# Two edits in the S5 stage of a diffusion block on one core: the state-space mixer's local table stays on the chip, and the modulation weights of the MLP scale are summed by TensorE ahead of the gated unit

## The chip, the cores and the metric

The kernel runs on one core of one Trainium2 chip. A core has five engines with instruction queues of their own: TensorE (PE in the rows; its weight loads are listed apart as PEld), VectorE (DVE), ScalarE (ACT), GpSimd (POOL) and SyncE (SP), which here only issues DMAs. Each queue is worked off in order. The metric is the device time in microseconds (us), median of several runs.

## What is computed

One block for a latent stream x of 256 tokens x 2048 channels, with a context of 256 tokens. Everything is float32, and the matrix weights are read once. Cut to what is run here:

```
sh1, sc1, gt1, sh2, sc2, gt2 = split(silu(c) @ w_mod + b_mod, 6)     # w_mod: 2048 x 12288; c_ctx the same
h = modulate(rmsnorm(x), sh1, sc1);   h_ctx likewise
# S5 mixer: 128 groups of 16 channels, 64 complex states per group, two directions
bu = einsum(u, b_bar);  states = scan(lam_bar, bu)                    # context first, then latent
y  = u * d + sum over directions of einsum(states, c_mat).real
a, g = split(gelu(y) @ w_glu);   m = a * sigmoid(g)                   # w_glu: 2048 x 4096
x = x + gt1 * rmsnorm(m)
h = modulate(rmsnorm(x), sh2, sc2)
x = x + gt2 * rmsnorm(relu(h @ w1)^2 @ w2)                            # 2048 x 8192, 8192 x 2048
```

The sixth of w_mod that gives sc2, the scale of the MLP's modulation, is one of the six 2048 x 2048 parts, 16 MB. The kernel calls it kind 4. Kinds 0 and 1 (the mixer's shift and scale, for c and c_ctx) are its "a" items, kind 2 is the mixer's gate, kind 3 the MLP's shift, kind 5 the MLP's gate.

## The kernel before

**Stages.** First the S5 stage, then the gated unit, then the MLP. The S5 stage works on 16 blocks `b` of 8 groups each, in three units of 4, 6 and 6 blocks (`UNITS`); a unit's recurrence runs as one scan. Weights come as items of 1 MB through one ring of tiles `raw` with three buffers (`RAWBUFS`), in one fixed order: 32 "a" items, then 32 "k" items of the kinds 3 and 2 between which the first ten items of the gated unit ("g", `GLU_EARLY`) are mixed (`MIX[n]` says how many k items stand before g item n), then 22 more g items, then the MLP. The ten early g items are multiplied in float32 straight from `raw`. The other 22 are split into a high and a low part by ScalarE and VectorE (`hi`, `lo`) and multiplied as three faster products; this is called the split stage below.

**One block of the S5 stage.** Its input tile `xv` (tiles xz0 to xz3, 4 blocks each) is multiplied with the row scale `rs` (`xn_blk`, L565) and then modulated with `vec` (`u_blk`, L569, two operations), once the "a" items of its chunk have been summed by TensorE (`a_mm`) and brought into columns (`vec_ev`, `vec_tr`, `vec_mask`, `vec_sel`, `vec_fin`). Chunks are 8, 8, 16, 32, 32 and 32 groups wide, so the last chunk feeds the last four blocks. From the discretised weights `bcb` come sums `s1e`, `s2e` (`e_sums`), and from these five operations of 512 elements per half block (`e_op`: k, e, e, and two sums), TensorE's transposes `tr`, ScalarE's copy `et`, and the matmul `v` (`v_mm`) that gives the scan its input. The scan is the chain `t`, `lat`, `lat` on VectorE (L727, L732, L734). After it ScalarE copies states (`sp_copy`), GpSimd adds two of them (`sp_sum`), VectorE makes three tables per half block (`d_op`, tiles dx), and TensorE makes the output `y` (`out_mm`) from the states and from the block's local response. `gelu` and the transpose `z_tr` follow.

**The local response.** It is a Toeplitz table: 15 diagonals of 16x16 per group. TensorE makes a strip from `e` and the block-diagonal output weights `cbd` (`strip`, L631), ScalarE copies it to `sk`, TensorE transposes it (`w_tr`), ScalarE and VectorE place it in `W` (`w_ev`, `w_diag`), SyncE writes `W` to DRAM (`w_out`) and reads it back eight times with a shift (`load_it`, 8 DMAs of 128 KB for each pair of blocks), and `out_mm` multiplies the tile `it` with `xv`.

**Engines.** Helper lines hide the work: every two-input operation made by `tt` stands at L122, every ScalarE copy at L125. In the S5 stage GpSimd does the row scale, the modulation of blocks 2 to 15, both kinds of sums and the last powers of the transition (`cmul(GP, ...)`).

**Kind 4.** Its 16 MB are loaded in the split stage into the two tiles xz0 and xz1 (`k4_load`), summed by VectorE with 16 operations of 2048 elements (`acc_op`, `acc_add`), and reduced over the partitions after the last split product by TensorE (`sc2_mm`, L1140), ScalarE (`row_ev`), TensorE (`col_mm`) and VectorE (`sc2_fin`).

**Order.** The order on each engine is fixed when the program is built: `Plan` takes all tasks with a cost, a priority, dependences and rings (counts of free buffers), simulates the engines, and emits each task when it is started in that simulation. A cost or ring that changes moves other tasks too.

Of the kernel before, what the change touches and what calls it, by code (L numbers as in the profile page):

```python
# [27 lines left out]
RAWBUFS = 3  # L28
# [9 lines left out]
MIX = (24, 26, 27, 29, 30, 32, 32, 32, 32, 32)  # L38
K4POS = ()
UNITS = (4, 6, 6)  # L40
PI = math.pi
# [75 lines left out]
def _body(ctx, tc, nc, I, O):  # L117
# [22 lines left out]
    shc = const.tile([128, 4, 4], F32, name="shc")  # L140

# [11 lines left out]

    k4v = KT - len(K4POS)
    kq = [kitem(kind, kt) for kind in (3, 2) for kt in range(KT)]
    nk = 0
    for n in range(len(GLU_ORDER)):
        m = MIX[n] if n < GLU_EARLY else nk + 2
        items += kq[nk:m]
        nk = max(m, nk)  # L160
        items.append(gitem(n))
        for j, at in enumerate(K4POS):
            if at == n:
                items.append(kitem(4, k4v + j))
# [64 lines left out]
    with psx:  # L229
# [15 lines left out]
        m16 = sb.tile([64, H], F32, name="m16")  # L245
        dcol = sb.tile([64, 32], F32, name="dcol")
# [34 lines left out]
        for dst, src in ((m16, "m16"), (dcol, "dcol"), (bcol, "bcol"), (sel4, "sel4")):  # L281
            S.dma_start(dst, I[src])
        V.memset(cst, 0.0)
        V.memset(epst, EPS)
        sk = ew.tile([128, L, 4, H], F32, name="sk")
        cbd = [ew.tile([128, 8, 2, 32], F32, name=f"cbd{n}") for n in range(2)]
        for t in cbd:
            GP.memset(t, 0.0)
# [42 lines left out]
        cm = {V: tmp("c0", [128, NB, 4, 8]), GP: tmp("c1", [128, NB, 4, 8])}  # L331
# [31 lines left out]
        cmul(GP, at(p_, 2), at(p_, 0), at(p_, 1))  # L363
        cmul(GP, span(p_, 4, 8), span(p_, 0, 4), rept(p_, 3, 4))
# [76 lines left out]
        def close_pre():  # L441
            nonlocal lp_, wk, drp
# [19 lines left out]
        for n in range(RB, min(nq + RB, len(items))):  # L462
            rawt[n] = add("SP", 2.91, lambda n=n: load_to(n + 1), prio=2, take=("raw",), lag=1.3)
# [1017 lines left out]
```

## Time and profile before

| | us |
|---|---|
| median of 3 runs (1309.31 to 1315.62) | 1313.72 |
| profiled execution | 1313.43 |
| its span, first to last instruction | 1311.7 |
| S5 stage with the early gated-unit items | 0 to 436 |
| of it up to the last step of the last scan | 0 to 386.9 |
| split stage of the gated unit | 436 to 559.3 |
| between gated unit and MLP | 559.3 to 586 |
| first MLP product | 586 to 943 |
| second MLP product and end | 943 to 1311.7 |

The boundaries are read from the timelines: where TensorE's first split product, the first product of the MLP and the first of its second half start. A row of a timeline gives start, duration, engine, line and tiles; a row of stretches gives the busy time of each engine between two times. Operations of one engine can overlap by a little in the rows, so the distance from start to start is what one costs (its pitch below), and the printed duration is longer.

### The profile page before, as it was taken

What the parts mean: (1) busy time and instruction counts of PE and PEld (TensorE: products, weight loads), DVE (VectorE), ACT (ScalarE), POOL (GpSimd) and SP (SyncE); (2) the same over time, 40 slices, a digit from 0 to 9 for tenths busy, and PEclk for the clock granted to TensorE, in tenths of its full rate; (3) what the DMA queues carried; (4) which work ended last, traced back from release to release, by engine and by line L of the source; (5) the groups of instructions that cost most, each with busy time, mean ns of one, the idle gap of its engine ahead of it and who ended that gap; (6) DMA issues with size and microseconds to landing.
All of it is one profiled execution on the core that took longest, in us unless ns stands there. A gap on an engine that the chain in (4) does not pass through costs nothing.

```text
span 1311.7 us, 22524 instructions
## 1 busy us (share of the span) xinstructions
PE 1178.7 (90%) x9457; PEld 957.2 (73%) x9457; DVE 897.1 (68%) x1200; ACT 539.4 (41%) x731; POOL 192.5 (15%) x200
## 2 busy tenths in 40 slices
PE   4576884696898999989999999999999999999997
PEld 1454553452434688989999999999978888888885
DVE  8999999878878677765555565555655555655555
ACT  5442544242115534574333334333434444444443
POOL 4766344611322000030000000000000000000000
PEclk8588997798899999999999999999999999999998
DMA  7488868989986888816656666566656555555552
GB/s 269 148 213 295 316 245 195 307 307 196 260 227 168 319 346 324 317 66 224 234 219 245 217 220 250 209 242 223 230 189 224 192 193 184 182 185 188 192 192 97
DMA packets 74093, 296.68 MB, mean 226 GB/s; under 512 B 7164, under 2 KB 30588, under 8 KB 48520
## 3 DMA queue, kind: packets, MB, share of 16 engines
q1 hardware_dynamic: 73992, 295.25, 66.3%
q8 instruction: 74, 1.21, 0.4%
q14 instruction: 27, 0.22, 0.1%
HBM read 291.15 MB, written 4.07 MB: 225 GB/s over the span
## 4 chain that ended last, share of the span: by engine, by line
PE 74%; DMA 9%; DVE 5%; SPq 1%; ACT 1%; issue 1%; POOL 0%; DVEq 0%; POOLq 0%; ACTq 0%
PE m L1325 27%; PE o L1358 27%; PE gb L998 9%; DMA raw<-wk 4%; PE gb L991 3%; DMA it<-wd 2%; DMA raw<-wa 2%; DVE e L122 2%; SPq L689 1%; PE ada L484 1%; PE y L800 1%; PE v L706 1%; DMA bcc<-bc 1%; PE m L1247 1%; PE ada L476 1%
## 5 line engine op out<-in xcount | busy, mean ns | idle before, releaser
L122 DVE TENSOR_TENSOR wlo<-raw,whi 128x2048 fp32r<-128x2048 f32 x126 | 288.7, 2291 | 134.7 <-ACT whi L125 134.7
L1325 PE MATMUL m<-h,whi 128*128 128x256 f32 x1984 | 248.2, 283 | 0.0
L125 ACT ACTIVATE whi<-raw 128x2048 fp32r<-128x2048 f32 (+1 forms) x130 | 243.8, 1876 | 1.5 <-PE m L1247 1.5
L1325 PEld LDWEIGHTS m<-h,whi 128*128 128x128 f32 x1984 | 242.5, 192 | 0.0
L1358 PE MATMUL o<-wlo,hh 128*128 128x512 f32 x512 | 160.5, 395 | 0.2 <-DVE wlo L122 0.2
L1358 PE MATMUL o<-whi,hh 128*128 128x512 f32 x512 | 160.6, 395 | 0.0
L1358 PE MATMUL o<-whi,hl 128*128 128x512 f32 x512 | 160.5, 395 | 0.0
L1325 PE MATMUL m<-h,wlo 128*128 128x256 f32 x992 | 129.1, 283 | 0.0
L1325 PEld LDWEIGHTS m<-h,wlo 128*128 128x128 f32 x992 | 123.5, 192 | 0.0
L125 ACT ACTIVATE hh<-hid 128x512 fp32r<-128x512 f32 x64 | 40.5, 633 | 194.5 <-PE o L1358 194.5
L125 ACT ACTIVATE r<-m 128x256 f32<-128x256 f32 x64 | 24.6, 384 | 222.9 <-PE m L1325 221.1
L1358 PEld LDWEIGHTS o<-wlo,hh 128*128 128x128 f32 x512 | 95.9, 187 | 24.1 <-DVE wlo L122 0.6
L1358 PEld LDWEIGHTS o<-whi,hh 128*128 128x128 f32 x512 | 95.8, 187 | 24.2 <-ACT hh L125 0.8
L1358 PEld LDWEIGHTS o<-whi,hl 128*128 128x128 f32 x512 | 96.0, 187 | 23.5
L1297 DVE TENSOR_TENSOR hl<-hid,hh 128x512 fp32r<-128x512 f32 x64 | 44.3, 693 | 88.8 <-ACT hh L125 88.7
L1269 DVE TENSOR_TENSOR hid<-r,m 128x256 f32<-128x256 f32 x64 | 26.9, 421 | 91.9 <-ACT r L125 91.9
L991 PE MATMUL gb<-raw,xz 128*128 128x512 f32 x160 | 76.0, 623 | 2.4 <-DMA raw<-wg 2.3
L623 PE MATMUL tr<-ident,e 128*128 128x128 f32 x256 | 44.7, 315 | 30.9 <-DVE e L122 24.6
L998 PE MATMUL gb<-hi,zs 128*128 128x512 f32 (+1 forms) x288 | 70.1, 357 | 0.0
L484 PE MATMUL ada<-raw,cst 128*32 128x512 f32 x256 | 36.9, 654 | 35.4 <-DMA raw<-wk 35.4
L623 PEld LDWEIGHTS tr<-ident,e 128*128 128x128 f32 x256 | 32.5, 160 | 45.8 <-DVE e L122 21.4
L991 PEld LDWEIGHTS gb<-raw,xz 128*128 128x128 f32 x160 | 30.2, 197 | 46.5 <-issue 40.2
(202 smaller groups left out, 1613.2 us busy)
## 6 DMA issues: line engine op xcount, KB each, us to landing
raw<-w SPq DMA_DIRECT2D x128, 1024.0 KB, 4.8
raw<-wk SPq DMA_DIRECT2D x48, 1024.0 KB, 8.4
raw<-wa SPq DMA_DIRECT2D x32, 1024.0 KB, 7.4
raw<-wg SPq DMA_DIRECT2D x32, 1024.0 KB, 5.2
k<-wk SPq DMA_DIRECT2D x16, 1024.0 KB, 7.3
it<-wd SPq DMA_DIRECT2D x64, 128.0 KB, 6.9
xz<-xs SPq DMA_DIRECT2D x4, 1024.0 KB, 9.1
bcb<-bc SPq DMA_DIRECT2D x16, 128.0 KB, 8.9
```

The lines of the kernel that those rows point to most:

```text
L122: eng.tensor_tensor(out=out, in0=a, in1=b, op=op)
L125: A.activation(out=out, in_=in_, func=f, **kw)
L476: PE.matmul(adab["a"][32 * j:32 * j + 32, :n], cst[:, 2 * kt:2 * kt + 32], w[:, e, j], start=(kt == 0), stop=(kt == KT - 1))
L484: PE.matmul(adab["k"][32 * j:32 * j + 32, :], cst[:, 2 * kt:2 * kt + 32], w[:, j * 512:(j + 1) * 512], start=(kt == k0), stop=(kt == KT - ...
L623: PE.transpose(est["ps"][:, gi * 128:(gi + 1) * 128], e[:, r, gi].rearrange("p s h -> p (s h)"), ident)
L689: S.dma_start(it[16 * s:16 * s + 16], wdt[b2][:, :, (7 - s) * H:(7 - s) * H + 128])
L991: PE.matmul(banks[p][nk * t + k], xz[kt // BQ][:, GQ * C + (kt % BQ) * T + t * 128:][:, :128], wt[:, (nk * e + k) * 512:(nk * e + k + 1) * ...
L998: PE.matmul(banks[p][nk * t + k][:, :wd], a, w[:, (nk * e + k) * wd:(nk * e + k + 1) * wd], start=ff, stop=ll)
L1269: V.tensor_tensor(out=hid[:, nt], in0=r, in1=ps, op=ALU.mult)
L1297: V.tensor_tensor(out=hl, in0=hid[:, 2 * i:2 * i + 2], in1=hh.bitcast(F32), op=ALU.subtract)
L1325: PE.matmul(ps, w[a][:, kt], (h2h, h2l)[b][:, kt], start=a == b == kt == 0, stop=a == 1 and kt == KT - 1)
L1358: PE.matmul(banks[nh][2 * t + k], w[2 + x][:, e, zz], w[y][:, e * 1024 + k * 512:e * 1024 + k * 512 + 512], start=f and n == 0 and e == es ...
```

## The change

- **Kind 4 becomes 16 more raw items.** They stand after kinds 3 and 2 in the list of k items, so that they are all loaded and multiplied ahead of the first split item, by `k_mm` like the others, four matmuls each. Row copy, `col_mm` and `sc2_fin` follow in the S5 stage. The loads into xz0 and xz1, VectorE's 16 sums and the reduction after the split stage are gone. `MIX` spreads the early g items over 48 k items.
- **RAWBUFS is 4** instead of 3.
- **The local response stays on the chip.** `strip` multiplies with zero-padded weights `cz` (one buffer), so that both halves of a block add up in one PSUM bank with all 15 diagonals; a matmul of a diagonal `dg` with `dsel` brings the skip term d. ScalarE copies the bank (`ext_ev`), TensorE makes the eight shifted copies by transposes (`t_tr`), ScalarE brings them into `it` (`t_ev`), and `yl_mm` multiplies at once with the block's `xv`; `yl_ev` writes the result over that half of `xv`. `out_mm` later adds it with one identity matmul. The strip, the transposes and `yl` of all blocks share one PSUM bank (`st`). The DRAM write and the 64 read-back DMAs are gone, as are `sk`, `W` and their copies.
- **GpSimd's work in the S5 stage goes to VectorE**: `xn_blk`, `u_blk`, `e_sums`, `d_sums`, `sp_sum` and the last powers. Some signs are turned so that sums replace differences.
- `gelu` comes after the transpose instead of before; the dx ring has 3 buffers instead of 4, k1 2 instead of 1, hf 2 instead of 4.
- The planner's costs of many tasks are changed.

```diff
-RAWBUFS = 3
+RAWBUFS = 4
...
-MIX = (24, 26, 27, 29, 30, 32, 32, 32, 32, 32)
-K4POS = ()
+MIX = (24, 26, 28, 32, 36, 40, 44, 48, 48, 48)
...
-    k4v = KT - len(K4POS)
-    kq = [kitem(kind, kt) for kind in (3, 2) for kt in range(KT)]
+    kq = [kitem(kind, kt) for kind in (3, 2, 4) for kt in range(KT)]
...
-            t = add("Pool", 1.23, lambda b=b: xn_blk(b), prio=3 + b, ready=28.7)
-            on_v = b < 2
-            ut[b] = add("DVE" if on_v else "Pool", 1.33 if on_v else 2.05, lambda b=b, e=V if on_v else GP: u_blk(b, e), [t, vect[chunk_of[b]]],
-                        prio=0 if on_v else 2 + b)
+            t = add("DVE", 0.61, lambda b=b: xn_blk(b), prio=PR["xn"])
+            ut[b] = add("DVE", 1.33, lambda b=b: u_blk(b, V), [t, vect[chunk_of[b]]], prio=PR["u"])
...
-            s1 = ew.tile([128, L, 8], F32, tag="s1e", bufs=2, name="s1e")
-            tt(SE, s1, Qr[:, b], Qi[:, b], ALU.add)
             s2 = ew.tile([128, 2, 8, H], F32, tag="s2e", bufs=1, name="s2e")
             tt(SE, s2[:, 0], Bv[:, 0], Bv[:, 1], ALU.add)
             tt(SE, s2[:, 1], Bv[:, 0], Bv[:, 1], ALU.subtract)
+            s1 = ew.tile([128, L, 8], F32, tag="s1e", bufs=2, name="s1e")
+            V.scalar_tensor_tensor(out=s1, in0=Qr[:, b], scalar=-1.0, in1=Qi[:, b], op0=ALU.mult, op1=ALU.subtract)
...
             k1, e = est[b, hf]
-            if k < 3:
-                o, p, c = ((k1, s1, Bv[:, 0]), (e[:, 1], Qr[:, b], s2[:, 0]), (e[:, 0], Qi[:, b], s2[:, 1]))[k]
-                tt(V, o, p[:, :, hs].rearrange("p t g -> p g t").unsqueeze(3).to_broadcast(n), c[:, hs].unsqueeze(2).to_broadcast(n), ALU.mult)
-            else:
-                tt(V, e[:, k - 3], k1, e[:, k - 3], ALU.subtract)
+            if k > 2:
+                tt(V, e[:, k - 3], k1, e[:, k - 3], ALU.add)
+                return
+            o, p, c = ((k1, s1, Bv[:, 0]), (e[:, 0], Qi[:, b], s2[:, 1]), (e[:, 1], Qr[:, b], s2[:, 0]))[k]
+            tt(V, o, p[:, :, hs].rearrange("p t g -> p g t").unsqueeze(3).to_broadcast(n), c[:, hs].unsqueeze(2).to_broadcast(n), ALU.mult)
...
+        def dg_op(b):
+            est["dg"] = dg = sb.tile([128, 128], F32, tag="dg", bufs=1, name="dg")
+            act(dg, ident, scale=dcol[:, b:b + 1])
+
         def strip(b, hf):
-            e = est[b, hf][1]
-            est["st", b, hf] = st = pst("st", 1)
-            for r in range(2):
+            k1, e = est[b, hf]
+            if hf == 0:
+                est["st", b] = pst("st", 1)
+                PE.matmul(est["st", b][:, :15 * H], est["dg"], dsel.rearrange("p s h -> p (s h)"), start=True, stop=False)
+            st = est["st", b]
+            for n, (r, w) in enumerate(((0, e[:, 0]), (1, e[:, 1]), (2, k1))[:3 if (b, hf) in PE_SUMS else 2]):
+                for d in range(2):
+                    for j in range(4):
+                        PE.matmul(st[32 * j:32 * j + 32, 7 * H * d:7 * H * d + 128], cz[:, d, r, j, hf * H:hf * H + 32], w[:, j].rearrange("p s h -> p (s h)"),
+                                  start=False, stop=(hf == 1 and n == (2 if (b, hf) in PE_SUMS else 1) and d == 1))
+
+        def ext_ev(b):
+            est["x1", b] = x = ew.tile([128, 15 * H], F32, tag="x1", bufs=2, name="x1")
+            act(x, est.pop(("st", b))[:, :15 * H], scale=-1.0)
+
+        def t_tr(b, th):
+
+            est["tp", b, th] = ps = pst("st", 1, "tp")
+            for i in range(4):
+                t = 4 * th + i
+                PE.transpose(ps[:, i * 128:(i + 1) * 128], est["x1", b][:, (7 - t) * H:(7 - t) * H + 128], ident)
+
+        def t_ev(b, th):
+            if th == 0:
...
+            act(est["it", b][:, 4 * th:4 * th + 4].rearrange("p t g h -> p (t g h)"), est.pop(("tp", b, th)))
...
+        def yl_mm(b):
+
+            est["yl", b] = ps = pst("st", 1, "yl")
+            yv = ps[:, :256].rearrange("p (t e h) -> p t e h", e=2, h=H)
+            for e in range(2):
                 for j in range(4):
-                    PE.matmul(st[32 * j:32 * j + 32, :128], cbd[b % 2][:, hf * 4 + j, r], e[:, r, j].rearrange("p s h -> p (s h)"),
-                              start=(r == 0), stop=(r == 1))
-
-        def strip_ev(b, hf):
-            lp = 2 * (b % 2) + hf
-            act(sk[:, :, lp], est.pop(("st", b, hf))[:, :128].rearrange("p (s h) -> p s h", h=H))
...
-        def w_tr(b2, hs):
...
-                PE.transpose(ps[:64, si * 128:si * 128 + 128], sk[:, s].rearrange("p l h -> p (l h)"), ident)
...
-        def w_ev(b2, hs):
...
-        def dd_mul(b2):
...
-        def w_diag(b2):
...
-        def w_out(b2):
-            wdt[b2] = wd = drp.tile([H, 16, 240], F32, tag="wd", bufs=8, name="wd")
-            S.dma_start(wd.rearrange("h (l j) f -> l h (j f)", l=4), wst[b2].rearrange("p j t h -> p (j t h)"))
-
...
-        def load_it(b2):
-            r = it_ring(b2)
-            itab[b2] = it = (lp_ if r == "it" else tail["whl"]).tile([128, 16, 128], F32, tag=r, bufs=1, name="it")
-            for s in range(L):
-                S.dma_start(it[16 * s:16 * s + 16], wdt[b2][:, :, (7 - s) * H:(7 - s) * H + 128])
+                    gi = 2 * j + e
+                    PE.matmul(yv[32 * j:32 * j + 32, :, e, :], xv[b // BQ][:, 0, (b % BQ) * 8 + gi], est["it", b][:, :, 2 * (gi % 4) + gi // 4, :], start=True, stop=True)
+
+        def yl_ev(b):
+            act(xv[b // BQ][:, 0, (b % BQ) * 8:(b % BQ) * 8 + 8].rearrange("p g c -> p (g c)"), est.pop(("yl", b))[:, :256])
...
-            sp, it = spt.pop(b), itab[b2]
+            sp = spt.pop(b)
...
+            PE.matmul(yb[b2][:, 256 * w:256 * w + 256], ident, xv[b // BQ][:, 0, (b % BQ) * 8:(b % BQ) * 8 + 8].rearrange("p g c -> p (g c)"), start=True, stop=False)
```

Where the order has changed, at three places. **VectorE right after the row scale is known.** Before, in this place (k and e: first block's tables; ARS: powers of the transition):

```order
L398 RECIPROCAL rs<-rs 128x64
L122 TENSOR_TENSOR k_319<-s1e,bcb 128x512
L122 TENSOR_TENSOR e<-Qr,s2e 128x512
L122 TENSOR_TENSOR e<-Qi,s2e 128x512
L429 COPY ARS<-pr 128x128
L430 COPY ARS<-pi 128x128
L122 TENSOR_TENSOR e<-k_319,e 128x512 x2
L438 COPY ARS<-ARS 128x128
L439 TENSOR_SCALAR ARS<-ARS 128x128
L122 TENSOR_TENSOR k_403<-s1e,bcb 128x512
```

and GpSimd at the same time (xz: the input blocks; rs: row scale; vec: modulation; s1e, s2e, s1d, s2d: sums for the tables):

```order
L122 TENSOR_TENSOR xz_75<-xz_75,rs 128x2x256 x4
L122 TENSOR_TENSOR s1e<-Qr,Qi 128x64
L122 TENSOR_TENSOR s2e<-bcb 128x128 x2
L122 TENSOR_TENSOR xz_76<-xz_76,rs 128x2x256 x4
L122 TENSOR_TENSOR xz_77<-xz_77,rs 128x2x256 x4
L122 TENSOR_TENSOR xz_78<-xz_78,rs 128x2x256
L122 TENSOR_TENSOR s1e<-Qr,Qi 128x64
L122 TENSOR_TENSOR s2e<-bcb 128x128 x2
L122 TENSOR_TENSOR xz_78<-xz_78,rs 128x2x256
```

Now, VectorE (pr, pi, c: powers; r and vec: modulation columns):

```order
L399 RECIPROCAL rs<-rs 128x64
L123 TENSOR_TENSOR xz_76<-xz_76,rs 128x2x256 x4
L123 TENSOR_TENSOR xz_77<-xz_77,rs 128x2x256 x4
L123 TENSOR_TENSOR xz_78<-xz_78,rs 128x2x256 x2
L510 TENSOR_TENSOR r_397<-vp,m_65 64x8 x4
L123 TENSOR_TENSOR xz_78<-xz_78,rs 128x2x256 x2
L522 TENSOR_TENSOR vec<-vp,rb 128x16 x2
L523 SCALAR_TENSOR_TENSOR vec<-vec,rb 128x16
L123 TENSOR_TENSOR xz_79<-xz_79,rs 128x2x256
L123 TENSOR_TENSOR xz_76<-xz_76,vec 128x2x256 x2
L123 TENSOR_TENSOR xz_79<-xz_79,rs 128x2x256 x3
L123 TENSOR_TENSOR s2e<-bcb 128x128 x2
```

The row scale of all 16 blocks, the sums and the powers now stand in VectorE's queue ahead of the first table.

**TensorE in the middle of the S5 stage**, around one block of the second unit. Before (tr: transposes of the tables; st: strip; wps: transposes of the strip; ada from raw: an "a" item; v: input of the scan):

```order
L623 MATMUL tr<-ident,e 128x128 x8
L636 MATMUL st<-e,cbd_145 32x128 x8
L476 MATMUL ada<-raw,cst 32x256 x8
L706 MATMUL v<-xz_77,et 64x64 x16
L636 MATMUL st<-e,cbd_145 32x128 x8
L476 MATMUL ada<-raw,cst 32x256 x8
L623 MATMUL tr<-ident,e 128x128 x8
L636 MATMUL st<-e,cbd_146 32x128 x8
L706 MATMUL v<-xz_77,et 64x64 x16
L476 MATMUL ada<-raw,cst 32x256 x8
L623 MATMUL tr<-ident,e 128x128 x8
L636 MATMUL st<-e,cbd_146 32x128 x8
```

Now (ada from raw: a k item; tp: shifted copies; yl: local part of the output):

```order
L659 MATMUL st<-dsel,dg 128x240
L664 MATMUL st<-e,cz 32x128 x16
L710 MATMUL v<-xz_77,et 64x64 x16
L485 MATMUL ada<-raw,cst 32x512 x4
L642 MATMUL tr<-ident,e 128x128 x8
L664 MATMUL st<-e,cz 32x128 x16
L710 MATMUL v<-xz_77,et 64x64 x16
L485 MATMUL ada<-raw,cst 32x512 x4
L676 MATMUL tp<-ident,x_2121 128x128 x4
L485 MATMUL ada<-raw,cst 32x512 x4
L676 MATMUL tp<-ident,x_2121 128x128 x4
L642 MATMUL tr<-ident,e 128x128 x8
```

The two strips of a block have 16 matmuls instead of 8, and one dsel matmul, eight tp transposes and the eight yl matmuls of the block stand between the tables of the next one; wps is gone.

**TensorE at the end of the S5 stage**, from the last k items on. Before (gb: early items of the gated unit; y: output of a block):

```order
L991 MATMUL gb<-raw,xz_77 128x512 x8
L991 MATMUL gb<-raw,xz_76 128x512 x8
L798 MATMUL y<-it,xz_77 32x8x16 x4
L800 MATMUL y<-dx,sp 32x8x16 x12
L798 MATMUL y<-it,xz_77 32x8x16 x4
L800 MATMUL y<-dx,sp 32x8x16 x12
L798 MATMUL y<-it,xz_77 32x8x16 x4
L800 MATMUL y<-dx,sp 32x8x16 x12
L798 MATMUL y<-it,xz_77 32x8x16 x4
L800 MATMUL y<-dx,sp 32x8x16 x12
L798 MATMUL y<-it,xz_78 32x8x16 x4
L800 MATMUL y<-dx,sp 32x8x16 x12
```

Now (ident: the identity that adds the local part; cp: the columns of kind 4, from evk):

```order
L485 MATMUL ada<-raw,cst 32x512 x12
L795 MATMUL y<-xz_78,ident 128x256
L802 MATMUL y<-dx,sp 32x8x16 x24
L485 MATMUL ada<-raw,cst 32x512 x4
L795 MATMUL y<-xz_78,ident 128x256
L802 MATMUL y<-dx,sp 32x8x16 x24
L533 MATMUL cp<-sel_66,evk 128x4 x4
L986 MATMUL gb<-raw,xz_77 128x512 x3
L795 MATMUL y<-xz_79,ident 128x256
L802 MATMUL y<-dx,sp 32x8x16 x24
L986 MATMUL gb<-raw,xz_78 128x512 x8
L795 MATMUL y<-xz_79,ident 128x256
```

The last k item and cp stand between the outputs of the last blocks, and each output has one matmul of 256 columns in place of the eight from `it`.

## Rows read from the trace of the kernel before

**Rows 1.** stretches: us, PE PEld DVE ACT POOL busy, PEclk, DMA, GB/s

```profile
0.00:386.90 386.90, 271.66 (x3688) 165.48 (x3689) 348.71 (x750) 141.38 (x298) 169.23 (x170) 0.85 0.83 250
386.90:436.00 49.10, 43.73 (x452) 21.78 (x450) 33.72 (x46) 26.79 (x32) 11.01 (x13) 1.00 0.66 192
436.00:559.30 123.30, 123.30 (x629) 103.56 (x632) 94.16 (x79) 55.48 (x76) 0.00 (x0) 1.00 0.85 328
...
586.00:943.00 357.00, 357.00 (x2977) 357.00 (x2976) 201.15 (x142) 135.95 (x125) 0.00 (x0) 1.00 0.62 227
```

**Rows 2.** the chain that ended last, between gated unit and MLP

```profile
560.36 0.60 ACT evg L125
```

**Rows 3.** timeline of VectorE: start, us, engine, line, operation; GpSimd idle

```profile
283.40 0.68 DVE L122 TENSOR_TENSOR e<-Qr,s2e 128x512 f32<-128x512 f32 x1
284.00 0.35 DVE L727 TENSOR_TENSOR t<-ARS,lat 128x192 f32<-128x192 f32 x1
284.27 0.68 DVE L122 TENSOR_TENSOR e<-Qi,s2e 128x512 f32<-128x512 f32 x1
...
286.41 0.35 DVE L727 TENSOR_TENSOR t<-ARS,lat 128x192 f32<-128x192 f32 x1
...
287.38 0.36 DVE L727 TENSOR_TENSOR t<-ARS,lat 128x192 f32<-128x192 f32 x1
```

**Rows 4.** timeline of GpSimd, one run of eight operations

```profile
154.99 10.66 POOL L122 TENSOR_TENSOR xz<-xz,vec 128x512 f32<-128x512 f32 x8 [3.40 <-DVE vec L522]
```

**Rows 5.** timeline of VectorE under that run: its first and last operation

```profile
155.57 1.08 DVE L734 TENSOR_TENSOR lat<-lat,t 128x64 f32<-128x64 f32 x1
...
165.73 0.81 DVE L122 TENSOR_TENSOR k<-s1e,bcb 128x512 f32<-128x512 f32 x1
```

**Rows 6.** waits of VectorE from 0 to 386.9: us in total, times, longest

```profile
DVE dx L122 <- PE y L800: 10.9, 3, 4.7
...
DVE xr L296 <- DMA are<-a_re: 2.4, 1, 2.4
DVE k L122 <- POOL s1e L122: 2.3, 2, 1.2
...
DVE rs L398 <- ACT rs L125: 1.9, 1, 1.9
```

**Rows 7.** timeline of TensorE around 260

```profile
259.68 1.93 PE L484 MATMUL ada<-raw,cst 128*32 128x512 f32 x8 [4.89 <-DMA raw<-wk]
...
266.76 1.09 PE L623 MATMUL tr<-ident,e 128*128 128x128 f32 x8
267.79 0.64 PE L636 MATMUL st<-e,cbd 128*32 128x128 f32 x16
268.25 1.04 PE L484 MATMUL ada<-raw,cst 128*32 128x512 f32 x8
```

**Rows 8.** groups by form, ScalarE, 0 to 436: count, busy us, mean ns

```profile
L125 ACT ACTIVATE et<-tr 128x512 f32<-128x512 f32 x64 | 36.4, 597 | 47.5 <-PE tr L623 43.7 <-PE v L706 3.2
```

**Rows 9.** waits of the SyncE queue over the whole span

```profile
SPq L254 <- ACT cbd L125: 54.9, 13, 11.7
```

**Rows 10.** timeline of the SyncE queue: first and thirtieth weight load

```profile
31.98 2.03 SPq L189 DMA_DIRECT2D raw<-wa  x2
...
183.36 2.65 SPq L189 DMA_DIRECT2D raw<-wk  x3
```

**Rows 11.** timeline of ScalarE after the last scan step

```profile
387.00 4.42 ACT L125 ACTIVATE sp<-lat 64x512 f32<-64x512 f32 x4 [10.99 <-DVE lat L734]
```

**Rows 12.** timeline of TensorE after the last scan step

```profile
391.26 0.42 PE L798 MATMUL y<-it,xz 128*32 128x128 f32 x8
...
393.03 0.40 PE L798 MATMUL y<-it,xz 128*32 128x128 f32 x8
...
402.96 7.13 PE L991 MATMUL gb<-raw,xz 128*128 128x512 f32 x16
...
426.00 1.12 PE L1036 MATMUL gp<-evg,ones 1*128 1x512 f32 x2
```

More of the change, by code (lines that the diff above doesn't have):

```diff
@@ L284, in _body @@
         V.memset(epst, EPS)
[L285 to L288, printed above, removed]
+        cz = ew.tile([128, 2, 3, 4, 3 * H], F32, name="cz")
+        GP.memset(cz, 0.0)
         def tmp(name, shape=None):
@@ L484, in k_mm @@
                 PE.matmul(adab["k"][32 * j:32 * j + 32, :], cst[:, 2 * kt:2 * kt + 32], w[:, j * 512:(j + 1) * 512],
-                          start=(kt == k0), stop=(kt == KT - 1 and kind != 4))
+                          start=(kt == 0), stop=(kt == KT - 1))
         def vec_ev(q):
@@ L815, in _body @@
             on_v = PR["sums"] == "DVE"
[L816 to L817 removed]
+            esum = add(PR["sums"], 0.42 if on_v else 1.1, lambda b=b: e_sums(b), ([bcl["b", b]] if b > 1 else []) + gate + (qt if b == 2 else []), prio=1, take=("s1e", "s2e"))
+            cs = [bcl["s", b]] if b > 1 else []
+            if sums(b):
+                cs = [add("DVE", 0.2, lambda b=b: c_sum(b), cs, prio=1)]
+            cb = add("ACT", 1.05 if sums(b) else 0.84, lambda b=b: c_diag(b), cs, prio=1, take=("cz",), give=("bcs",))
+            dg = add("ACT", 0.28, lambda b=b: dg_op(b), prio=1, take=("dg",))
             for hf in range(2):
@@ L882, in _body @@
         swp = virt(swap, etasks)
-        for b2, wo in itw.items():
-            itt[b2] = add("SP", 4.72, lambda b2=b2: load_it(b2), [wo, swp], prio=1, take=("it2",), lag=2.0)
         for b in range(NB):
@@ L1089, in _body @@
             z_split(b2)
-        for kt in range(k4v):
-            ring = ("xz0", "xz1")[kt % 2]
-            ld = add("SP", 2.91, lambda kt=kt: k4_load(kt), list(zst.values()), prio=PR["k4l"], take=(ring,), lag=1.3)
-            acct = [add("DVE", 2.26, lambda kt=kt: acc_op(kt), [ld, end5] + acct, prio=PR["acc"], give=(ring,))]
         stagger = [(4, 2), (4, 3)]
-        k4t = []
         for key in queue:
-            if key[0] == "k" and key[1] == 4:
-                kt = key[2]
-                k4t.append(add("PE", 0.91, lambda kt=kt: k_mm(4, kt), [rawt[order_n[key]]] + k4t[-1:], prio=PR["k4"], take=("ada",) if kt == k4v else (), give=("raw",)))
             if key[0] != "g":
@@ L1132, in _body @@
                 evict(p)
-        def sc2_mm():
-            if not k4t:
-                adab["k"] = pst("ada", 1)
-            for j in range(4):
-                PE.matmul(adab["k"][32 * j:32 * j + 32, :], tail["ones"][:, 0:32], tail["acc"][:, j * 512:(j + 1) * 512], start=not k4t, stop=True)
-        def sc2_fin():
-            s2f = tail["sc2"].rearrange("p m j -> p (m j)")
-            V.tensor_tensor(out=s2f, in0=adab["cp"][:, :16], in1=bcol[:, 1], op=ALU.add)
-            V.scalar_tensor_tensor(out=s2f, in0=s2f, scalar=1.0, in1=bcol[:, 2], op0=ALU.add, op1=ALU.mult)
         def stat_sum(t, k, lo, n):
@@ L1237, in _body @@
             for h in range(2):
-                x = add("ACT", 0.95, lambda key=key, h=h: w_hi(key, h), [rawt[len(queue) + n]] + acct + [(y, 0.0) for y in hs], prio=2, take=() if h else ("mw",))
+                x = add("ACT", 0.95, lambda key=key, h=h: w_hi(key, h), [rawt[len(queue) + n]] + [(y, 0.0) for y in hs], prio=2, take=() if h else ("mw",))
                 hs = [x]
```

242 lines of the change are left out of this document (109 added, 133 removed).

## The prediction

> **What bounds the kernel now.** I read the stretches first. In the split stage TensorE is busy 123.30 of 123.30 us and in the first MLP product 357.00 of 357.00 [rows 1], with the same matmuls in both kernels; no edit to other engines can shorten these as long as TensorE stays fed. So the S5 stage decides, 0 to 436. Up to the last scan step (386.9) VectorE is busy 348.71 us and TensorE 271.66 [rows 1]; the reader is to see there that VectorE sets the pace. After it, TensorE is busy 43.73 of 49.10: it makes the last outputs and early gated-unit items. The time is therefore: when does the last scan end, and how much TensorE work is left then.
>
> **What a VectorE operation costs.** The timeline of VectorE with GpSimd idle gives 0.60 us from start to start for 512 elements (283.40 to 284.00) and 0.27 for 192 (284.00 to 284.27), so about 0.07 us + 1.03 ns per element [rows 3]. An operation that needs the one just ahead costs about 0.12 more: a scan step of 192, 96 and 96 elements takes 0.97 alone (286.41 to 287.38) and 0.27 + 0.17 + 0.17 = 0.61 when other work stands between [rows 3]. Priced so, VectorE's list before, up to the last scan step, comes to 288.9 us. It was busy 348.7 [rows 1], so 60 us are stretch. GpSimd's runs show where from: during its eight operations of 10.66 us [rows 4] VectorE got through nine operations from 155.57 to 165.73 [rows 5] (four of 512, two of 128, three of 64 elements) that are worth 3.2 us at the pitches. They alternate. Idle time is 386.9 - 348.7 = 38 us; 4.3 of it is at the start (2.4 for are, 1.9 for rs), 10.9 waits for y, 2.3 for GpSimd's s1e [rows 6].
>
> **GpSimd's work to VectorE.** In the changed order GpSimd has nothing to do between its first memsets and the MLP, so the 60 us of stretch go. VectorE gains, up to the last scan step: 16 row scales x 0.60 = 9.6; 28 modulations x 0.66 (every second waits for the one ahead) = 18.5; 32 s2e x 0.20 = 6.4; 16 s1e x 0.13 = 2.1; 26 s2d x 0.20 and 13 s1d x 0.13 = 6.9; 10 state sums of 256 x 0.34 = 3.4; six operations of the powers, 3.9; less the 16 W additions and with small differences, -1.3. Together +49.5, so 338.4 us. At the stretched prices that was 349, so the exchange itself gives 10 us; more comes only if waits shrink.
>
> **The waits.** 338.4 + 4.3 at the start = 342.7 without any other wait. Before, 34 us of waits stood beside the start. GpSimd's 2.3 goes [rows 6]. The y waits (10.9: a dx buffer is free only when TensorE has used it) can grow, as the dx ring has one buffer less and TensorE has more to do. Bounds: 10 us (half the rest hidden) and 50 (TensorE's queue adds to them). I take 30, near what before had, so the last scan ends at **373**. A second way gives the same: the last four blocks need the last chunk of "a" items. VectorE's list up to there is 127 us, + 4.3 + some 10 of waits = 142; the DMAs, from 32 [rows 10] with 28 more items at 3.2 us (1 MB at the split stage's 328 GB/s [rows 1]) = 122, plus the small loads between, 132 to 143. From there 211 us of list and 20 of waits: 373.
>
> **The table without DRAM, and kind 4, on TensorE.** Prices at full clock (the rows count two records for a matmul, one for a transpose): 8 strip matmuls 0.46 (267.79 to 268.25), a k item 1.0 (1.04 for its four matmuls), a transpose of 128 columns 0.13 (x8 records, 266.76 to 267.79, is 1.03 for eight of them by the order) [rows 7], 512 columns 0.89 (7.13 for 8) [rows 12]. Added: kind 4, 16 x 1.0 = 16; strips, 32 x 0.46 = 15; dsel, 240 columns, 16 x 0.42 = 7; tp, 128 x 0.13 = 17, less 64 wps = -8; identity, 256 columns, 16 x 0.45 = 7; yl costs what the removed matmuls from it cost. Sum 53 (61 at the clock before, 0.85 up to 386.9). TensorE's 271.7 + 43.7 = 315.4 [rows 1], less the four gp matmuls that now stand in the split stage, 4.2 (1.12 for one, 1.05 of pitch [rows 12]), become 364 to 372. In a stage of 416 that is 88%, against 72% before: hidden under VectorE, but with less room. If that cover goes, kind 4 costs its 16 us in full. In the split stage it gives nothing back (123.30 of 123.30), and its 16 VectorE sums there were hidden.
>
> The DMAs: before, 250 GB/s x 387 + 192 x 49 [rows 1] = 106 MB in the stage. Kind 4 adds 16.8, the table's write and read-back (64 x 128 KB and the writes) take off some 10: 113 MB in 416 us, 271 GB/s, below the 328 of the split stage. What is queued behind: k items stand in TensorE's queue among tr and v, so one that lands late holds the next block's tables; the small loads stand in SyncE's queue among the items (below).
>
> **The one PSUM bank.** Per block: strips 2 x 0.92, dsel 0.42, tp 1.0, yl 0.5, and on ScalarE two copies of 512 at 0.60 [rows 8] and two half as long, 5.6 in all; between the halves five table operations with the scan between, 3 to 4.4; some eight hand-overs and places in TensorE's queue. Estimate 11 to 13 us. VectorE's list has 161 us from block 4's tables to block 15's, 14.6 per block, so the bank should follow. Where blocks are closest in the order (10.3 per block, 8 to 10) it can't quite; that is in the 30.
>
> "Mind PSUM pressure: TensorE tiling speeds up compute but not PSUM evacuation", says the Trainium skill, Trainium Kernel Development and Optimization, Best Practices; no row of before shows this bank as the last wait, and were it so, at 18 us per block the last scan would end near 404 and the time be 1329.
>
> **After the last scan.** ScalarE's copies for the first block, 2 x 1.1 (4.42 for four [rows 11]), the sum 0.35 and hand-overs: 3.2. Then TensorE, by the order: six blocks y at 1.77 (391.26 to 393.03), 32 early items' matmuls at 0.89 = 28.5 [rows 12], one k item and cp, 2: 44.3, against 49.1 - 4.2 = 44.9. Gain 0.6. Then the copy evg, 0.60 [rows 2], falls out of the chain between gated unit and MLP: 0.6.
>
> **Sum.** 373 - 386.9 = -13.9, -0.6, -0.6: -15 to the profiled run's 1313.43, which is its median (1313.72) within 0.3: **1298 us**.
>
> **The rivals.**
>
> TensorE becomes the bound. For it: 372 us of work in an in-order queue that waits for tables, copies and DMAs; at the low clock a k item takes 1.93 instead of 1.04 [rows 7]. Against: the clock was 1.00 where TensorE was dense (386.9 to 436), 0.85 where it wasn't [rows 1], so more work should lift it. It decides if TensorE idles over 45 us of the stage; before it idled 121. At 60 us the split stage starts at 432, and the time is 1309.
>
> The weights come late: slower. SyncE's queue is in order, and before it stood 54.9 us behind the small loads whose buffer ScalarE's cbd copies hadn't freed [rows 9]; now there is one cz where there were two cbd, so a load of the next block waits for the strips of the one before. Before, 29 items took from 31.98 to 183.36, 5.2 us each [rows 10]. At that price the last chunk is ready at 188, and 211 + 20 us follow: 419, so 1344. Against: before, items were also held by three buffers, now four, and TensorE takes an item as soon as it stands. It is slower than before from 4.2 us per item on (last chunk after 156).
>
> Almost no waits: 342.7 + 10, so 1278. For it: the DRAM round trip, GpSimd's hand-overs and their waits are gone.
>
> The change doesn't do what it says: the stretch isn't GpSimd's but, say, the DMAs'. Then 338 + 60 + 34 = 432, and 1357. Against: the pitch is 0.60 where GpSimd is idle [rows 3], in a stage in which the DMAs are busy 0.83 of the time [rows 1].
>
> The Trainium skill, SBUF — State Buffer, section SBUF: two separate sides, says that DMAs can't slow an engine's access, and that VectorE and GpSimd lock one pair of ports, the loser blocked for the whole instruction. The alternation in the trace agrees (3.2 us of work in 10.2); by the rule this rival falls, by the rows alone I keep a small chance.
>
> **How the numbers follow.** A difference under 0.5% (6.6 us) is about what can't be told from none. Forecast 0.52 (0.50 faster, 0.02 same); TensorE bound 0.17 (0.05, 0.11, 0.01 slower); late weights 0.12 (0.02 same, 0.10 slower); almost no waits 0.13, faster; stretch stays 0.06 (0.01 same, 0.05 slower). Faster 0.68, same 0.16, slower 0.16. The range, 1276 to 1320, runs from the case of almost no waits to weights at 4.4 us per item (last chunk at 160, last scan at 391); beyond lie the rest of the late weights and the stretch that stays, and a little below.
>
> **What would show it.** Right: 512-element operations at 0.60 in all of the S5 stage, the last scan step near 373, 44 us from there to the split stage, no SyncE wait of over some us before the last "a" item, the split stage at 123 + 4 with gp. Wrong: TensorE dense from 150 on with VectorE waiting for tr, st or y (bound), "a" loads 4 us or more apart (late), or pitches over 0.7 (stretch).

## The result and the profile after

The changed kernel takes 1281.82 us (median of 4 runs, 1280.33 to 1282.46); the kernel before, on the same chip, 1314.55. The ratio is 0.9757, 95% interval 0.9729 to 0.9785. The forecast was 1298 with a range of 1276 to 1320: the time is inside, the sign is right, but the gain of 33 us is twice the forecast one of 15.

The stretches of the changed kernel (us, PE, PEld, DVE, ACT, POOL busy, PEclk, DMA share, GB/s), cut where the last scan step ends, the first split product starts, the last one ends, and the MLP's first main product starts and ends:

```profile
0.00:353.70 353.70, 305.28 (x4517) 184.38 (x4517) 330.00 (x884) 156.69 (x314) 1.26 (x5) 0.94 0.77 288
353.70:399.00 45.30, 44.36 (x389) 23.09 (x389) 32.05 (x60) 25.06 (x30) 0.95 (x1) 0.95 0.57 212
399.00:527.50 128.50, 128.50 (x634) 104.44 (x632) 64.34 (x69) 57.98 (x80) 0.00 (x0) 1.00 0.57 206
527.50:553.40 25.90, 21.47 (x163) 20.78 (x163) 17.05 (x34) 19.83 (x55) 11.52 (x16) 0.93 0.01 2
```

Against [rows 1] the whole gain is in the first line: the last scan step ends at 353.7 instead of 386.9, 33.2 us earlier. The rest cancels out: 45.3 us from there to the first split product (before 49.1, of which 4.2 were the gp matmuls that now stand later), 128.5 for the split stage with its 4.2 us of gp (123.3 + 1.0), 25.9 for the join (between gated unit and MLP, to the MLP's first main product) instead of 26.6, 0.6 less at the end. GpSimd is idle. TensorE is busy 305 of the first 354 us, at a granted clock of 0.94 instead of 0.85.

VectorE's waits in the first stretch (us in total, times, longest):

```profile
DVE e L123 <- PE st L664: 8.0, 3, 4.0
DVE xr L297 <- DMA are<-a_re: 2.7, 1, 2.7
DVE rs L399 <- ACT rs L126: 1.9, 1, 1.9
DVE r L510 <- PE vp L498: 1.3, 1, 1.3
DVE dx L123 <- PE y L802: 1.2, 2, 0.7
```

The 10.9 us for y of [rows 6] are down to 1.2, and of the small loads only the one at the start (are, 2.7) is still waited for. The wait of e for the strip has grown from 2.8 us in the kernel before to 8.0; e's buffers come free when the strip's matmuls have read them, and whether the one PSUM bank or TensorE's queue holds these was not taken apart. The timeline of VectorE shows the modulation columns of the last chunk ready at 139.3 and 512 elements at 0.60 (145.80 to 146.40) beside a busy TensorE and busy DMAs:

```profile
139.27 0.22 DVE L523 SCALAR_TENSOR_TENSOR vec<-vec,rb 128x64 f32<-128x64 f32 x1
...
145.80 0.68 DVE L123 TENSOR_TENSOR e<-Qr,s2e 128x512 f32<-128x512 f32 x1
146.40 0.21 DVE L736 TENSOR_TENSOR lat<-lat,t 128x64 f32<-128x64 f32 x1
```

The rest of the way, on the chain that ended last, is TensorE's: gb, y, then the split products.

```profile
368.23 7.06 PE gb L986 x16
375.73 1.45 PE y L802 x48
...
390.77 8.78 PE gb L986 x20
399.55 1.40 PE gb L993 x6
...
553.41 357.12 PE m L1289 x2976
```

In the kernel before, the same chain ran from 395 to 416.6 over other engines: seven issues of read-backs on SyncE (395.0 to 400.3), a late small load, GpSimd's sum and VectorE's last tables.

```profile
400.72 5.98 DMA bcc<-bc
406.83 0.97 POOL s2d L122
408.68 6.38 DVE dy L122 x9
```

### The profile page after: what moved, and what is told of

It is laid out like the page before. It is cut to its first block, busy times and chain, and to the rows that moved or that the text cites. A ratio compares the mean times of both kernels' runs of the same rounds, so it can differ in the third digit from the quotient of the medians.

```text
span 1278.6 us, 23766 instructions
## 1 busy us (share of the span) xinstructions
PE 1216.6 (95%) x10217; PEld 977.3 (76%) x10217; DVE 847.3 (66%) x1336; ACT 555.1 (43%) x747; POOL 14.7 (1%) x23
## 4 chain that ended last, share of the span: by engine, by line
PE 78%; DVE 17%; DMA 2%; ACT 2%; issue 1%; POOL 0%; DVEq 0%; SPq 0%; ACTq 0%
PE m L1289 28%; PE o L1322 28%; PE gb L993 9%; PE gb L986 5%; DVE e L123 4%; DVE dx L123 2%; DVE xz L123 2%; PE y L802 1%; DVE t L731 1%; DMA raw<-wa 1%; PE ada L478 1%; PE v L710 1%; DVE k L123 1%; PE ada L485 1%; DVE t L734 1%; DVE lat L738 1%
## 5 line engine op out<-in xcount | busy, mean ns | idle before, releaser
L993 PE MATMUL gb<-lo,zs 128*128 128x512 f32 (+1 forms) x208 | 61.1, 359 | 0.0
L993 PEld LDWEIGHTS gb<-hi,zs 128*128 128x128 f32 x288 | 49.7, 188 | 12.0 <-issue 3.3
L485 PE MATMUL ada<-raw,cst 128*32 128x512 f32 x384 | 54.0, 638 | 4.5 <-DMA raw<-wk 4.5
L126 ACT ACTIVATE sp<-lat 64x512 f32<-64x512 f32 x32 | 35.6, 1113 | 50.3 <-DVE lat L738 25.8
```

Source lines behind the costliest of these rows:

```text
L126: A.activation(out=out, in_=in_, func=f, **kw)
L485: PE.matmul(adab["k"][32 * j:32 * j + 32, :], cst[:, 2 * kt:2 * kt + 32], w[:, j * 512:(j + 1) * 512], start=(kt == 0), stop=(kt == KT - 1))
L993: PE.matmul(banks[p][nk * t + k][:, :wd], a, w[:, (nk * e + k) * wd:(nk * e + k + 1) * wd], start=ff, stop=ll)
```

## Experiments

The change is three edits and a buffer: the table on the chip (T), GpSimd's work on VectorE (G), kind 4 on TensorE (K), and the fourth raw buffer (R). Each ratio is to the kernel before, run on the same chip. "Last scan" is the end of the last scan step and "split" the start of the first split product, both from the timelines; the four gp matmuls (4.2 us) stand ahead of that start in before, e1, e3, e4 and e5, and behind it in the changed kernel.

| run | what is in it | us | ratio to before (95%) | last scan | split |
|---|---|---|---|---|---|
| before | none | 1314 (1312 to 1315 in the groups of runs) | 1 | 386.9 | 436 |
| e6 | T | 1308.0 | 0.9967 (0.9946 to 0.9988) | 381.5 | 425.8 |
| e3 | G | 1328.3 | 1.0107 (1.0083 to 1.0132) | 398.8 | 446.8 |
| e4 | K | 1346.7 | 1.0251 (1.0228 to 1.0274) | 384.8 | 469.0 |
| e1 | T, K, R | 1304.5 | 0.9927 (0.9907 to 0.9947) | 371.9 | 428.9 |
| e5 | T, G, K | 1294.0 | 0.9866 (0.9829 to 0.9903) | 352.4 | 413.1 |
| e2 | T, G, R | 1282.9 | 0.9763 (0.9737 to 0.9788) | 352.6 | 402.0 |
| after | T, G, K, R | 1281.8 | 0.9757 (0.9729 to 0.9785) | 353.7 | 399.0 |

Alone, T gains 6 us, G costs 14 and K costs 33; together, with R, they gain 33. T is what is left when the others are taken back: it keeps the planner's new costs and s1e and the last powers on VectorE; G in e3 leaves the powers on GpSimd. Each edit also moves the planner's order, so a row is an edit with its order. The sections below say how much of this is shown.

### e1 and e3: GpSimd's work back, and GpSimd's work alone

e1 is the changed kernel with these lines, and sums='Pool', spsum='Pool':

```diff
-            tt(V, x, x, rs.rearrange(...
+            tt(GP, x, x, rs.rearrange(...
-            t = add("DVE", 0.61, lambda b=b: xn_blk(b), prio=PR["xn"])
-            ut[b] = add("DVE", 1.33, lambda b=b: u_blk(b, V), [t, vect[chunk_of[b]]], prio=PR["u"])
+            t = add("Pool", 1.23, lambda b=b: xn_blk(b), prio=3 + b, ready=28.7)
+            on_v = b < 2
+            ut[b] = add("DVE" if on_v else "Pool", ...
```

e3 is the kernel before with the opposite edit.

> The changed kernel with the row scale, the modulation of blocks 2 to 15, s2e, both d sums and the state sums on GpSimd again (powers and s1e stay on VectorE). Theory A, GpSimd stretches VectorE: VectorE's list falls to about 295 us but is stretched by some 50, so the last scan step moves from 353.7 to about 363 and the time to about 1291. Rival, the stretch is not GpSimd's (DMA traffic): the list runs at its short pitches, the last scan comes earlier than 353.7 until TensorE binds near 340, time about 1268.

> The kernel before with only GpSimd's row scale, modulation, sums and state sums on VectorE (table through DRAM, three raw buffers and kind 4 as before). Theory B, the waits beside the list came from the table's way through DRAM: list about 338, 5 at the start and some 25 of waits as before, last scan near 368, time about 1295. Theory A, the waits came with GpSimd's hand-overs: some 10 of waits, last scan near 354, time about 1281.

Measured: e1 1304.5. The last scan moves back to 371.9, not forward: GpSimd's stretch is real (theory A), though the scan came 9 and the end 13 us later than reckoned. In the presence of T, K and R, G is worth 22.7 us. VectorE was busy 343.8 us up to the last scan step, against 330.0 in the changed kernel: the exchange itself gave 13.8 us.

e3 came out at 1328.3, slower than before and slower than either theory said. VectorE is no longer stretched, and is busy less up to the last scan step (336.1 against 348.7 [rows 1]), but it idles 62 us:

```profile
0.00:398.50 398.50, 272.87 (x3705) 161.60 (x3705) 336.11 (x893) 140.95 (x298) 32.10 (x26) 0.86 0.81 247
```

```profile
DVE s2d L122 <- DMA bcc<-bc: 23.1, 6, 5.9
DVE sp L122 <- ACT sp L125: 6.1, 6, 1.5
DVE r L509 <- PE vp L497: 5.1, 2, 3.8
DVE W L671 <- ACT W L125: 4.7, 3, 2.5
```

The largest wait is new: the sums s2d, now in VectorE's queue, wait 23.1 us for the small load bcc. In the kernel before the same operations waited for the same loads on GpSimd, where it cost little (VectorE waited 2.3 us for GpSimd's sums [rows 6]; groups by form, GpSimd):

```profile
L122 POOL TENSOR_TENSOR s2d<-bcc 128x128 f32<-128x128 f32 x32 | 27.1, 867 | 50.3 <-DMA bcc<-bc 43.1 <-DVE lat L732 7.2
```

So an engine with room had absorbed late loads, and moving its work handed the waiting to the engine that sets the pace. Theory B, that the waits come with the table's way through DRAM, is the nearer one, but it had 25 us of waits.

### e8 and e9: what makes the small loads late

e8 is e3, with the eight shifted read-backs of a pair replaced by one load of the same size from an input; the local part of the output is left out that way:

```diff
-            for s in range(L):
-                S.dma_start(it[16 * s:16 * s + 16], wdt[b2][:, :, (7 - s) * H:(7 - s) * H + 128])
+            S.dma_start(it.rearrange("p a b -> p (a b)"), I["xs"][b2 // 2])
```

e9 is e3 with the planner's number for the landing of small loads as in the changed kernel: lag=2.0 becomes lag=5.0.

> The run with only GpSimd's work moved, but the table is not read back: each pair's tile it is loaded with one DMA of 1 MB from an input, the same bytes in one transfer of long rows (the local part of the output is left out that way). Theory, the 64 shifted read-backs of short rows hold the other loads: the 27 us of VectorE's waits for bcc go and the last scan comes near 368, 1295 to 1300. Rival, the order is to blame (the planner reckons 2 us from issue to landing of these loads): no change, 1323 to 1333.

> The run with only GpSimd's work moved, with one number changed: the planner reckons 5 us instead of 2 from issue to landing of the small loads, as the changed kernel does. Theory, the order is to blame: VectorE's waits for bcc fall below 10 us and the time to about 1310. Rival, the read-backs are: waits stay near 27 us, time 1323 to 1333.

e8: 1300.1 (ratio 0.9905, 0.9874 to 0.9937), the last scan at 371.7. e9: 1327.9 (1.0111, 1.0085 to 1.0138), as e3. The waits of VectorE for bcc, first in e8 up to its last scan step, then in e9 up to 400:

```profile
DVE s2d L122 <- DMA bcc<-bc: 3.1, 1, 3.1
```

```profile
DVE sp L122 <- ACT sp L125: 17.5, 9, 8.1
DVE r L509 <- PE vp L497: 9.1, 3, 4.2
DVE s2d L122 <- DMA bcc<-bc: 7.6, 4, 3.1
```

In e9 the order allows for late loads and the bcc wait falls to 7.6, as the theory said, but other waits grow and the time stays, so the order alone is not to blame. In e8 the same bytes come in long rows, and 28 us are gone. The page's line on packets, e3 first, then e8:

```profile
DMA packets 74091, 296.67 MB, mean 224 GB/s; under 512 B 7164, under 2 KB 30588, under 8 KB 48520
```

```profile
DMA packets 57836, 296.66 MB, mean 229 GB/s; under 512 B 6269, under 2 KB 13309, under 8 KB 31241
```

The bytes are the same, 16,255 packets fewer. e8 also has 8 issues on SyncE in place of 64 (5.71 us for eight read-backs at 319 in the kernel before), and its loads need not wait until the table's write has landed: in e3 SyncE stood 12.1 us ahead of read-backs until a DMA ended, in e8 no such wait is listed. The three weren't taken apart: it is the read-backs, by their rows, their issues or their wait for the write.

### e7: what GpSimd costs VectorE

The changed kernel with idle work for GpSimd:

```diff
         V.reciprocal(out=rs, in_=rs)
+        junk = sb.tile([128, 512], F32, name="junk")
+        GP.memset(junk, 0.0)
+        tt(GP, junk[:, :64], rs, rs, ALU.add)
+        for n in range(64):
+            tt(GP, junk, junk, junk, ALU.add)
```

> The changed kernel with 64 additions of 512 elements on GpSimd that nobody uses, back to back from the row scale on. Theory, GpSimd stretches VectorE: some 90 us of GpSimd time cost VectorE 0.36 to 0.66 us each, 30 to 60 us, so 1312 to 1342, with VectorE's pitch of 512 elements above 0.8 while they run. Rival, the stretch of before was DMA traffic: pitch stays 0.60, time 1282.

1329.7 us, ratio 1.0129 (1.0103 to 1.0154). Timeline of GpSimd, and under it two groups of VectorE by form (busy, mean ns) while it runs, the second from the changed kernel:

```profile
27.68 89.16 POOL L123 TENSOR_TENSOR junk<-junk 128x512 f32<-128x512 f32 x64
```

```profile
L123 DVE TENSOR_TENSOR e<-k,e 128x512 f32<-128x512 f32 x8 | 11.9, 1522 | 0.0
```

```profile
L123 DVE TENSOR_TENSOR e<-k,e 128x512 f32<-128x512 f32 x21 | 13.6, 684 | 0.0
```

89.2 us of GpSimd move the last scan step from 353.7 to 403.3: 49.6 us, 0.56 for each us of GpSimd. The rival (DMA traffic) is out: nothing but GpSimd's work and the one tile was added, and the same operation takes 1.52 instead of 0.68.

### e2, e4, e11 and e5: kind 4 and the fourth buffer

e2 is the changed kernel with the code of before for kind 4 (`k4_load`, `acc_op`, `sc2_mm`), with `kq` and MIX of before; e4 is the kernel before with the new code for kind 4, in the order 3, 4, 2 of the kinds for want of a row tile. e11 is e4 with the plain load of e8, again without the local part of the output. e5 is the changed kernel with RAWBUFS = 3.

```diff
-    kq = [kitem(kind, kt) for kind in (3, 2) for kt in range(KT)]
+    kq = [kitem(kind, kt) for kind in (3, 4, 2) for kt in range(KT)]
```

> The changed kernel with kind 4 as before: 16 MB into xz0 and xz1 in the split stage, summed by VectorE, reduced after the last split product. Theory: kind 4's 16 us of TensorE in the S5 stage lie under VectorE, so taking them out gives nothing: 1281 to 1283. Rival, TensorE (94 per cent busy from 200 us on) already sets the end of the S5 stage: up to 16 us faster, about 1266.

> The kernel before with only kind 4 moved to raw items that TensorE sums in the S5 stage (order of kinds 3, 4, 2). Theory: TensorE idles 121 us of that stage, so it is hidden: 1311 to 1316. Rival, its 16 us and 16 MB push the late k items and early gated-unit items: up to 16 us slower, about 1329.

> The kernel before with only kind 4 moved (the run at 1346.7), and each pair's tile it loaded with one DMA of long rows from an input instead of the eight shifted read-backs (the local part of the output is left out that way). Theory, kind 4 is dear there because the DMAs are full with short rows (busy share 0.99 from 300 to 400): the k items come in time, 1305 to 1318. Rival, it is dear because of TensorE's 16 us or the three buffers: 1335 to 1347.

> The changed kernel with three raw buffers instead of four. Theory, the weights run ahead of VectorE, so the fourth buffer is worth little: 1281 to 1287. Rival, the last chunk of a items comes late again (188 us in the kernel before, 139 in the changed one): with every 10 us of it the time rises by 10, to 1300 and more.

e2 is at 1282.9 against 1281.8: beside T, G and R, kind 4 on TensorE is hidden, it neither gives nor costs. e4 is slower by 33, more than the rival's 16. e11 comes back by 24 (by 20 between the profiled runs), to 1323.2 (1.0095, 1.006 to 1.0131), between the two theories. e5 is at 1294.0: the fourth buffer is worth 12 us (10 between the profiled runs), but not where the rival had it; the last chunk is as early as with four (columns ready at 138.9). In e4 and e5 the last scan step hardly moves; what grows is the stretch behind it (rows: e4, then e5, then e11; columns as above):

```profile
384.80:469.00 84.20, 73.09 (x579) 31.39 (x578) 29.80 (x42) 26.57 (x33) 10.87 (x13) 0.94 0.79 267
```

```profile
352.40:413.10 60.70, 55.77 (x437) 25.60 (x429) 34.21 (x64) 27.67 (x34) 0.95 (x1) 0.94 0.68 251
```

```profile
372.40:449.00 76.60, 68.94 (x577) 29.89 (x569) 28.40 (x41) 26.31 (x32) 10.73 (x13) 0.96 0.78 292
```

TensorE is busy 73 us behind e4's last scan step, where it was 44 in the kernel before [rows 1]: twelve k items and 91 records of early gated-unit matmuls (60 before) were left over. From 300 to 400 the DMAs are full in e4 and not in e11:

```profile
300.00:400.00 100.00, 75.04 (x719) 35.48 (x720) 77.55 (x179) 24.34 (x25) 21.97 (x27) 0.86 0.99 268
```

```profile
300.00:400.00 100.00, 82.68 (x964) 40.35 (x966) 86.49 (x185) 28.84 (x29) 36.80 (x36) 0.90 0.79 291
```

But full DMAs are not what makes kind 4 dear there. e11 has room in them, and behind its last scan step stand the same twelve k items: 577 records against 579, 76.6 us against 84.2, where the kernel before had 49.1. What the long rows gave is the last scan step, 12.4 us earlier, and 7.6 of the stretch behind it. The rest lies in the order. Only two of the twelve items stand ahead of the first output y of the last unit in TensorE's queue; ten stand behind it, with 80 records of the gated unit (48 in the kernel before), and that y needs the last scan. They have to wait for it whenever their weights come: ten items at 1.0 us and 16 matmuls more at 0.89 are some 24 us behind the last scan. The order is fixed when the program is built, and it is the same in e4 and e11: `Plan` reckons 4.72 us of SyncE for each `load_it` in both. In the changed kernel one k item stands behind that y, in e5 four, so the three buffers are part of it; what in the plan puts the others there is open. What long rows would give without kind 4 wasn't run; beside G they gave 28 (e3, e8).

The waits of VectorE for y up to the last scan step, in e4 and e11, then in e6 and e1:

```profile
DVE dx L122 <- PE y L804: 11.8, 4, 4.7
```

```profile
DVE dx L122 <- PE y L803: 0.6, 1, 0.6
```

```profile
DVE dx L123 <- PE y L804: 9.8, 4, 4.7
```

```profile
DVE dx L123 <- PE y L804: 1.8, 1, 1.8
```

With one order (e4, e11) the wait goes with the read-backs. Yet e6, which has no read-backs either, has nearly as much; e1, with kind 4 and the fourth buffer on top, has 1.8. So taking out the read-backs was not enough.

e6 is e1 with kind 4 on VectorE and three buffers: of the change only the table, with the planner's new costs.

> The changed kernel with GpSimd's work back (but powers and s1e on VectorE), kind 4 back on VectorE and three raw buffers: of the change only the table on the chip (and the planner's new costs) is left. Theory: kind 4 cost nothing beside the table, so this is the run with GpSimd back again: 1302 to 1307. Rival, the fourth buffer matters to the arrival of the weights: 1310 to 1318.

1308.0, between the two: T alone is worth 6 us. VectorE idles 37.1 of its 381.5 us up to the last scan step, nearly as in the kernel before (38.2).

### e12 and e13: a faster version?

Both use the changed kernel's own switch by which TensorE adds k and e, two VectorE operations less per half block; e12 on the basis of e2.

```diff
-PE_SUMS = ()
+PE_SUMS = tuple((b, h) for b in (4, 6, 8, 10, 12, 14) for h in range(2))
```

e13 has the blocks 6, 10 and 13.

> The changed kernel with kind 4 back on VectorE in the split stage, and with TensorE adding k and e for the tables of six blocks (12 half blocks: two VectorE operations less in each, six sums of 256 elements more). Theory, VectorE is the bound of the S5 stage: 24 x 0.6 less, 2 more, last scan near 341 and 1271. Rival, TensorE (some 18 us more, kind 4's 16 less) is as near to the bound: 1280 to 1286.

> The changed kernel, kind 4 on TensorE, with TensorE adding k and e for three blocks (6 half blocks). Theory, VectorE is the bound: 12 x 0.6 less, 1 more, so 6 us earlier, 1276. Rival, TensorE at 94 per cent from 200 us on gives them back (9 us more on TensorE): 1282 to 1288.

1291.7 (0.9854, 0.9814 to 0.9894), slower than either theory said, and 1287.9 (0.9823, 0.9788 to 0.9857), the rival's: both slower than without. The stretch from 100 to 300, e2 first, then e12, and e12's waits of VectorE up to its last scan step (360.4):

```profile
100.00:300.00 200.00, 180.85 (x2885) 117.31 (x2884) 193.52 (x500) 101.28 (x209) 0.00 (x0) 0.97 0.66 249
```

```profile
100.00:300.00 200.00, 186.68 (x3198) 129.89 (x3190) 179.69 (x473) 104.57 (x209) 0.00 (x0) 0.97 0.67 250
```

```profile
DVE e L123 <- PE st L664: 11.2, 4, 4.6
...
DVE dx L123 <- PE y L802: 4.3, 2, 4.1
```

VectorE's work fell by 13.8 us, as meant, and its idle time rose by as much; TensorE had 6 us more, with 11.2 us of waits for the strip and 4.3 for y. TensorE is busy 185.1 of these 200 us in the changed kernel, 185.8 in e13 and 186.7 in e12, so it is likely the second bound; the one bank of the strip would make the same wait, and the two weren't taken apart. No version here beats the changed kernel.

## Why the forecast was right, and where its size was off

- **VectorE bounds the stage, GpSimd stretches it.** Right: 512 elements at 0.60, GpSimd idle; e7 shows the stretch by itself, at 0.56 us per GpSimd us. The rival that it isn't GpSimd's is out.
- **The list, 338.4 us.** Right: with 4.6 us of waits at the start (xr, rs) and 10.5 others (e, r, dx) it makes 353.5, measured 353.7. It holds the 330.0 us that VectorE is busy and some 8 us of short gaps, idle time (23.7) that the listed waits (15.9) don't explain.
- **The last chunk at 142.** Right: 139.3, with 7.7 us of waits ahead of it (e, r) where the forecast had 10. The late-weights rival didn't come, although SyncE stood 70 us behind the copies into `cz` in the first 400. The a items were issued from 26.9 to 122.5; why they ran on, the fourth buffer can't have been (e5 has 138.9 with three).
- **The waits, 30 us, near what before had.** This term failed; it was 10. From 139.3 the last scan took 214 us, against a list of 211: 3 us of waits where I had 20. The term was too large in two ways. First, about 8 us were counted twice. VectorE's idle time before, 38.2 us, has 30.4 of listed waits; the other 7.8 are short gaps, the same as in the changed kernel, and the list of 338.4 already holds them. So the exchange gave more than the 10 us of the forecast (VectorE is busy 18.7 us less), and there was less to carry over than the 34. Second, the listed waits were not a property to be carried over: they fell from 30.4 to 15.9 (18.7 + 14.5 are the 33.2). Where they went is shown in part. With one order the read-backs make them: without them e4's wait for y falls from 11.8 to 0.6 and its last scan comes 12.4 us earlier (e11), e3's wait for bcc falls from 23.1 to 3.1 (e8). But in e6, without read-backs, the wait for y was still 9.8; that it is 1.2 in the changed kernel takes the other edits and their order, and which of them is open. The case that came true is the rival "almost no waits" (1278), held at 0.13; that the time lies inside the range is owed to that rival being its lower end.
- **Kind 4 is hidden.** Right in the changed kernel (e2), but the forecast's reason, TensorE's spare time (busy 88% of the stage), is not enough: the kernel before had more of it (busy 72%), and there the same edit costs 33 us (e4). There the order puts ten k items behind an output that needs the last scan. The forecast had read from the changed order that it is one there, and didn't say that its cover hangs on that. The DMA rates in the forecast, 271 GB/s against 328, counted bytes alone; e4's DMAs were full at 268.
- **The fourth buffer** had no term in the sum. It is worth 10 to 12 us (e5), behind the last scan.
- **The tail and the join.** 45.3 against 44.3 forecast, 0.7 gained against 0.6. The split stage is 1.0 longer and the end 0.6 shorter, for which the sum had no term; they happen to cancel.
- **TensorE as the bound** didn't come true, but was likely near: in e12 some more of its work, in place of kind 4's, already went with as many waits as VectorE had gained. The forecast's price for this rival, 1309, left out the gp matmuls' 4.2 us in the split stage; with them it is 1313.

## What to carry to other kernels

Before carrying a wait over to a changed order, ask which resource makes it, and whether the change removes that resource. Work on an engine with room also absorbs late loads; moved to the engine that sets the pace, it brings its waits along, and pays only once the loads come in time. Edits that use up slack (16 more items, more work for VectorE) should be tried with the edit that makes the slack, since alone they can cost what together they gain. And where a program fixes the order, look behind what a piece of work stands in its queue: spare time that lies ahead of it is of no use.

## What the hardware showed

Two-input operations of VectorE and GpSimd took turns: 89.2 us of GpSimd cost VectorE 49.6 us (e7). Where both had operations of 512 elements, each finished one every 1.45 us (VectorE's start at 71.55, 73.00 and 74.44; GpSimd's eleven from 59.50 on take 15.91). The Trainium skill, SBUF — State Buffer, section SBUF: two separate sides, tells of an exclusive lock for a whole instruction; the trace agrees in kind, 1.52 us in place of 0.68 being longer by less than one GpSimd operation of 1.39.

64 read-backs of 128 KB in short rows, behind the write that they need, cost 28 us more than the same bytes in eight loads of 1 MB from an input (e3, e8), and 20 to 24 in another order (e4, e11). From 300 to 400 the DMAs were busy 0.99 at 268 GB/s with them and 0.79 at 291 GB/s without (e4, e11).
